# Squares of x added up in PSUM by VectorE, with the rotary angles, their sines and the low-rank Tanh emitted at other places

## The chip, the cores and the metric

One core of one Trainium2 chip runs the whole kernel. The metric is the device time of one execution in microseconds (us); less is better. Its engines are TensorE (PE, with its weight loads as PEld), VectorE (DVE), ScalarE (ACT), GpSimd (POOL) and SyncE (SP), whose queue issues all transfers. Each engine works through its own list in order and waits at semaphores for the others.

## The reference

One encoder layer with 1024 positions and a model width of 1024. What bears on this change is its beginning:

```python
h = rms_norm(x, norm_mix_g[l])                 # x * rsqrt(mean(x*x) + eps) * g
proj = h @ w_in[l]
mla_cols, rw_cols, gate_cols = _split(proj, [MLA_COLS, RWKV_COLS, GATE_COLS])
...
ang = positions.astype(jnp.float32)[..., None] * inv_freq
cos, sin = jnp.cos(ang).astype(x.dtype), jnp.sin(ang).astype(x.dtype)
...
q_rope = rope(rms_norm(q_rope, qr_g), cos[:, :, None, :], sin[:, :, None, :])
k_rope = rope(rms_norm(k_rope, kr_g), cos, sin)
...
a = jax.nn.sigmoid(a0 + a_lo @ a2)
w = -jax.nn.softplus(-(w0_d + jnp.tanh(dlo) @ w2_d)) - 0.5
```

Attention over all positions, a forward and a backward RWKV-7 scan, two output projections and a gated feed-forward layer follow.

## The kernel before, in words

Activations lie as features by positions, [128, 1024], in two halves of 512 positions (`HT`), each half one PSUM bank wide. Every product is made to nearly float32 accuracy by splitting both operands into a high and a low part: `whi` is a ScalarE cast of a weight tile, `wlo` the rest, computed by GpSimd, and each pair of halves takes six matmuls, hh*whi, hl*whi and hh*wlo for both halves. One "k step" below is such a group of six for one of the eight 128-row slices of x.

**The first stage** loads eight tiles `xt` of x. `ld` makes `hh` (ScalarE, x times the gain) and `hl` (VectorE, the rest). The reciprocal norm `rstd` isn't applied to x but to the products, when they leave PSUM (`evac`), so matmuls can start before it is known. `square(k)` squares a tile on ScalarE, and GpSimd adds the squares up in `acc` (named `xacc` in the trace). Step "s" of the list `XORDER` sums `acc` over the features with two float32 matmuls (`ss<-xacc`), and ScalarE makes `rstd` from it with a Ln and an Exp. `XORDER` also sets the order of TensorE's work: the tiles `T_CQ` (two) and `T_CKV`, with "s" between the second and the third. `rotary_tables` computes the angles of the rotary embedding on VectorE: some 18 instructions on [128, 1024], from a broadcast load of the positions, ending in a ScalarE Sin for `sinT` and one for `cosT`.

**The second stage** is one after another `inproj(T_L2)`, `inproj(T_L1)`, `inproj(T_GF)`, `inproj(T_GB)` and twelve more tiles. Their PSUM banks are three called `st` and one called `po`: `T_CQ` holds all four, so `T_L2`, which takes two of them, waits for `evac` of `T_CQ`. `l1_done` and `l2_done` shift the low-rank columns (tiles `l1` and `l2`) and put a Tanh on half of each. Between the k steps stand pieces of background generators: `norm_ckv`, `norm_cq`, `key_rope` (rotary key, tiles `sqk` and `rsk`, needs `cosT` and `sinT`), `rw_prep(p)` for four pairs of heads (first step "lora": matmuls `up<-l,a2w` and `up<-l,w2b`, then a ScalarE Sigmoid into `at` or `sg`), `mla_nope` (matmuls `up<-ck`, then `lift`: a Square `sqh` on ScalarE and a copy `q` on VectorE, then the sum `ss<-ghi`, `ss<-glo`), `mla_v` and `mla_rope`. Background products share two PSUM banks called `up`, sums share two called `ss`.

**The order.** TensorE's list is the order in which the program emits matmuls. Where a background piece stands is set by a clock that the program counts itself (`now`): a generator yields a name, and the table `DELAY` says how long after that its next piece may be emitted. The other engines' lists in these stages are made by the scheduler of the language, from dependences and its own estimates. From the scan on, all lists are written by hand.

A ScalarE function belongs to a table set, and `act` puts a table load where the set changes: Ln and Exp share one, Sigmoid and Tanh another, Sin a third. Squares, copies and scalings need none.

Of the kernel before, what the change touches and what calls it, by code (L numbers as in the profile page):

```python
# [54 lines left out]
CARRY = 3000  # L55
BATCH = 2500
DELAY = {
    "tab": 2100, "sum": 3900, "cq": 2040, "kr": 3100, "kr2": 750, "kr3": 0, "nope": 2975, "nope2": 1440,
    "rope": 541, "rope2": 5334, "rope3": 1470, "v": 805, "lora": 746, "kk": 10600, "kk2": 1785, "rk": 4080,
    "bo": 400,  # L60
}
# [25 lines left out]
def block_kernel(ctx: ExitStack, tc: tile.TileContext, a):  # L87
# [183 lines left out]
    onef = ap_.tile([128, 128], F32, name="onef")  # L271
    G.memset(onef, 1.0)
    G.tensor_copy(onesr, onef)
    HT = (slice(0, 512), slice(512, 1024))

    nst = [0]
# [27 lines left out]
    cqps = [big(), big()]  # L304
    ckps = [up1(), up1()]
    first3 = [*cqps, ckps]
    with pool("xp") as xp:
        xt = [xp.tile([128, T], F32, name=f"xt{k}") for k in range(8)]
        acc = xp.tile([128, T], F32, name="xacc")
        w3 = {}  # L310

        def wl3(t, h):
            raw = xp.tile([128, 512], F32, tag=f"raw{t}", name=f"raw{t}{h}")
            nc.sync.dma_start(raw, a["w_in"][t][:, h * 512:(h + 1) * 512])
            if h == 0:
                hi, lo = (xp.tile([128, 512], R, name=f"{n}{t}") for n in ("whi", "wlo"))
            else:
                hi, lo = (wpool["w"].tile([128, 512], R, tag=n, name=n, bufs=2) for n in ("whi", "wlo"))
            split(raw, hi, lo)
            w3[t, h] = hi, lo  # L320

        def ld(k):
            nc.sync.dma_start(xt[k], a["xT"][k * 128:(k + 1) * 128, :])
            hh, hl = hx[k]
            S.activation(hh, xt[k], AF.Copy, scale=vc("gmix", k))
            V.scalar_tensor_tensor(out=hl, in0=xt[k], scalar=vc("gmix", k), in1=hh.bitcast(F32), op0=mult, op1=sub)

        def square(k):
            if k == 0:
                S.activation(acc, xt[0], AF.Square)  # L330
            else:
                S.activation(xt[k], xt[k], AF.Square)
                G.tensor_tensor(out=acc, in0=acc, in1=xt[k], op=add)

        def mm(t, k):
            wh, wl = w3[t, k // 4]
            ws = slice(k % 4 * 128, (k % 4 + 1) * 128)
            mmk(first3[t], wh[:, ws], wl[:, ws], hx[k], k == 0, k == 7)

        def rotary_tables():  # L340
            posi = xp.tile([128, T], I32, name="posi")
            nc.sync.dma_start(posi, a["pos"].to_broadcast([128, T]))
            ang, kq = (xp.tile([128, T], F32, name=n) for n in ("ang", "kq"))
            V.tensor_copy(ang, posi)
            V.tensor_scalar(ang, ang, cst[:, C_FREQ:C_FREQ + 1], None, op0=mult)
            magic = 12582912.0
            for dst, off, fin in ((sinT, 0.0, 0.0), (cosT, 0.25, 0.5 * math.pi)):
                V.tensor_scalar(kq, ang, 1.0 / (2 * math.pi), off, op0=mult, op1=add)
                V.tensor_scalar(kq, kq, magic, -magic, op0=add, op1=add)
                src = ang  # L350
                rest = 2 * math.pi
                for bits in (8, 8, 8, 24):
                    if bits == 24:
                        cc = float(np.float32(rest))
                    else:
                        m, e = math.frexp(rest)
                        cc = math.ldexp(math.floor(m * 2 ** bits), e - bits)
                    rest -= cc
                    V.scalar_tensor_tensor(out=dst, in0=kq, scalar=-cc, in1=src, op0=mult, op1=add)
                    src = dst  # L360
                pi_ = 3.1415925
                if fin:
                    V.tensor_scalar(dst, dst, fin, pi_, op0=add, op1=ALU.min)
                    V.tensor_scalar(dst, dst, -pi_, None, op0=ALU.max)
                else:
                    V.tensor_scalar(dst, dst, pi_, -pi_, op0=ALU.min, op1=ALU.max)
                act(dst, dst, AF.Sin)

        for step in XORDER:
            if step[0] == "w":  # L370
                wl3(step[1], step[2])
            elif step[0] == "x":
                ld(step[1])
            elif step[0] == "q":
                square(step[1])
            elif step[0] == "r":
                rotary_tables()
            elif step[0] == "m":
                mm(step[1], step[2])
            else:  # L380
                for hs in HT:
                    ss = ss1()
                    E.matmul(ss, onef, acc[:, hs], start=True, stop=True)
                    rsqrt_(rstd[:, hs], ss, 1.0 / D, eps)
# [18 lines left out]

    for q, ps in zip([*cqs, ckv], first3):
        evac(q, ps)

    nc.sync.dma_start(a2w, a["w_l1"])
    for dst, src in ((b64r, a["consts"][:, C_B64:]), (b16, a["b16"])):
# [71 lines left out]
    def norm_cq():  # L480
        sq = [tt("sq") for _ in range(2)]
        for i in range(2):
            S.activation(sq[i], cqs[i], AF.Square)
        G.tensor_tensor(out=sq[0], in0=sq[0], in1=sq[1], op=add)
        pt = parted2(sq[0])
        yield "sum"
        rs = tt("rs")
        for x, hs in zip(pt, HT):
            rsqrt_(rs[:, hs], gsum(onesr, x), 1.0 / 256, eps)
        for i in range(2):  # L490
            V.scalar_tensor_tensor(out=cqs[i], in0=cqs[i], scalar=vc("gqa", i), in1=rs, op0=mult, op1=mult)
            split(cqs[i], cqh[:, i, :], cql[:, i, :], V)
        yield "cq"
# [143 lines left out]
    def rw_prep(p):  # L637
        cs = slice(p * 128, (p + 1) * 128)
        w2b = tp.tile([64, 128], F32, tag="w2b", name="w2b", bufs=2)
        nc.sync.dma_start(w2b, a["w_l2"][:, cs])  # L640
        at = keep(3, "at")
        for dst, wt, src, bias, key in (
            (at, a2w[0:64, cs], l1[0:64, :], vc("a0", p), None),
            (None, a2w[64:128, cs], l1[64:128, :], vc("w0f", p), "s0"),
            (None, w2b, l2[0:64, :], vc("w0b", p), "s1"),
        ):
            if dst is None:
                dst = tt("sg")
            for hs in HT:
                ps = up1()  # L650
                mul(ps, wt, src[:, hs], start=True, stop=True)
                act(dst[:, hs], ps, AF.Sigmoid, bias=bias)
                yield "lora"
            if key:
                nc.sync.dma_start(d_rw[key][:, p, :], dst)
        yield (p, 1)
        kt = rkv[p, 1]
        sq = tt("sq")
        S.activation(sq, kt, AF.Square, scale=vc("kk", p))
        pt = parted2(sq)  # L660
        kf = tt("kf")
        S.activation(kf, at, AF.Identity, scale=vc("ka", p), bias=ka1[:, p:p + 1])
        G.tensor_tensor(out=kf, in0=kf, in1=kt, op=mult)
        for h in range(2):
            nc.sync.dma_start(d_rw[("x2", "x1")[h]][H[h], p, :], kf[H[h], :])
        yield "kk"
        nr = tt("nr")
        for x, hs in zip(pt, HT):
            V.tensor_scalar(nr[:, hs], gsum(b64r, x), 1e-24, None, op0=ALU.max)
        act(nr, nr, AF.Ln, scale=float(2.0 ** KK_SHIFT))  # L670
        act(nr, nr, AF.Exp, scale=-0.5, bias=kkb)
        V.scalar_tensor_tensor(out=nr, in0=kt, scalar=vc("kk", p), in1=nr, op0=mult, op1=mult)
        nc.sync.dma_start(d_rw["kk"][:, p, :], nr)
        V.scalar_tensor_tensor(out=at, in0=at, scalar=-1.0, in1=nr, op0=mult, op1=mult)
        for h in range(2):
            nc.sync.dma_start(d_rw[("x1", "x2")[h]][H[h], p, :], at[H[h], :])
        yield "kk2"
        yield (p, 0)
        rk = kf
        V.scalar_tensor_tensor(out=rk, in0=rkv[p, 0], scalar=vc("rk", p), in1=kf, op0=mult, op1=mult)  # L680
        pt = parted2(rk)
        yield "rk"
        yield (p, 2)
        bo = tt("bo")
        for x, hs in zip(pt, HT):
            bs = gsum(b64r, x)
            V.tensor_tensor(out=bo[:, hs], in0=bs, in1=rkv[p, 2][:, hs], op=mult)
            yield "bo"
        S.activation(bo, bo, AF.Identity, bias=vc("lnb", p))
        nc.sync.dma_start(d_rw["bo"][:, p, :], bo)  # L690
# [11 lines left out]

    def l1_done(ps):
        shift(ps, 0, l1)
        act(l1[64:128, :], l1[64:128, :], AF.Tanh)

    def l2_done(ps):
        shift(ps, 1, l2)
        act(l2[0:64, :], l2[0:64, :], AF.Tanh)

    def gl_done(d):
        def done(ps):
# [1475 lines left out]
```

## Time and profile before

| | us |
|---|---|
| median of 3 runs | 1938.6 (1937.78 to 1941.22) |
| the profiled execution | 1937.92 |
| its span, first to last instruction | 1936.1 |
| TensorE busy in the span | 1841.8 (95%) |
| VectorE, ScalarE, GpSimd busy | 1229.6, 871.1, 655.4 |

The profiled execution lies 1.8 us above its span and 0.7 us below the median. A busy TensorE also counts time in which it ran at a lower clock; the granted clock is a column of the view of windows (1.00 is 2.4 GHz, 0.50 is 1.2 GHz).

### The profile page before, as it was taken

Reading aid. Unit: us, or ns where it says so; the run is one execution under the profiler, and the core shown is the slowest. Engines: PE = TensorE matmul, PEld = TensorE weight load, DVE = VectorE, ACT = ScalarE, POOL = GpSimd, SP = SyncE. Lnnn points to the kernel's source line nnn. Section 1 sums busy time; section 2 is a strip of 40 time slices with the busy share of each in tenths; the row PEclk is TensorE's granted clock in tenths of the full one; section 3 lists DMA queues with packets and bytes.
Section 4 is the critical chain, followed back from the end, with each engine's and each line's share of the span. In section 5 each row is a group of like instructions: output and inputs, shape, how many; then the busy total and the mean of one; then the engine's idle time right before and its main releaser. Section 6 shows DMA issues by size and latency. Waiting matters only on the chain. (4 is left out here: it accounts for less than half of the span.)

```text
span 1936.1 us, 36734 instructions
## 1 busy us (share of the span) xinstructions
PE 1841.8 (95%) x14928; PEld 1467.8 (76%) x14928; DVE 1229.6 (64%) x1837; ACT 871.1 (45%) x1380; POOL 655.4 (34%) x558
## 2 busy tenths in 40 slices
PE   6889999999999999989999999988999999999998
PEld 5657666888788877767777777767888888888886
DVE  7567665445556686766573264687766757667567
ACT  5676567223233565655666444442323333233231
POOL 7435554421222333352533322236222222222321
PEclk9989999999999999997999999999999999999999
DMA  4135544954555645453435672101111111111112
GB/s 158 37 120 193 181 157 147 252 140 99 142 144 122 148 110 137 101 139 84 104 83 174 213 250 87 55 33 55 50 56 59 49 50 52 63 50 50 49 55 103
DMA packets 260632, 210.65 MB, mean 109 GB/s; under 512 B 127144, under 2 KB 205032, under 8 KB 260464
## 3 DMA queue, kind: packets, MB, share of 16 engines
q1 hardware_dynamic: 260464, 208.31, 36.4%
q8 instruction: 117, 1.92, 0.4%
q14 instruction: 51, 0.42, 0.1%
HBM read 144.64 MB, written 59.41 MB: 105 GB/s over the span
## 5 line engine op out<-in xcount | busy, mean ns | idle before, releaser
L108 POOL TENSOR_TENSOR wlo<-wraw,whi 128x512 fp32r<-128x512 f32 x118 | 162.2, 1375 | 586.9 <-ACT whi L108 580.1
L123 PE MATMUL st<-hh,whi 128*128 128x512 f32 x408 | 172.4, 422 | 15.1 <-ACT hh L108 9.5
L123 PE MATMUL st<-hl,whi 128*128 128x512 f32 x408 | 163.6, 401 | 0.7 <-DVE hl L108 0.7
L108 DVE TENSOR_TENSOR x<-b,x 128x512 f32<-128x512 f32 x176 | 119.0, 686 | 54.9 <-PE b L123 54.9
L123 PE MATMUL st<-hh,wlo 128*128 128x512 f32 x408 | 140.3, 398 | 0.7 <-POOL wlo L108 0.7
L108 POOL TENSOR_TENSOR pl<-pe,ph 128x512 fp32r<-128x512 f32 x64 | 83.1, 1300 | 165.3 <-ACT ph L108 154.6
L108 ACT CAST whi<-wraw 128x512 fp32r<-128x512 f32 x118 | 72.9, 618 | 110.3 <-issue 30.4
L123 PEld LDWEIGHTS st<-hh,whi 128*128 128x128 f32 x408 | 78.9, 193 | 43.6 <-issue 10.9
L108 DVE TENSOR_REDUCE mx<-sc 128x1 f32<-128x512 f32 x128 | 81.8, 682 | 28.3 <-PE sc L123 28.1
L123 PEld LDWEIGHTS st<-hh,wlo 128*128 128x128 f32 x408 | 78.4, 192 | 19.1 <-POOL wlo L108 1.5
L123 PEld LDWEIGHTS st<-hl,whi 128*128 128x128 f32 x408 | 79.1, 194 | 17.7 <-DVE hl L108 1.6
L108 POOL TENSOR_TENSOR wl<-wraw,wh 128x512 fp32r<-128x512 f32 x22 | 28.9, 1313 | 179.7 <-ACT wh L108 174.8
L108 DVE TENSOR_TENSOR u<-b,p 128x512 f32<-128x512 f32 x42 | 29.0, 690 | 71.7 <-PE b L123 71.7
L123 PE MATMUL b<-sh,wh 128*128 128x512 f32 x176 | 69.3, 394 | 2.6 <-ACT sh L108 2.6
L123 PE MATMUL b<-sl,wh 128*128 128x512 f32 x176 | 69.1, 393 | 0.8 <-DVE sl L108 0.8
L123 PE MATMUL b<-sh,whi 128*128 128x512 f32 x176 | 68.6, 390 | 1.3 <-DVE x L108 1.3
L123 PE MATMUL b<-sh,wl 128*128 128x512 f32 x176 | 69.2, 393 | 0.0
L123 PE MATMUL b<-sh,wlo 128*128 128x512 f32 x176 | 68.5, 389 | 0.0
L123 PE MATMUL b<-sl,whi 128*128 128x512 f32 x176 | 68.5, 389 | 0.0
L108 DVE TENSOR_TENSOR pl<-st,ph 128x512 fp32r<-128x512 f32 x64 | 43.6, 683 | 28.3 <-ACT st L108 27.9
L108 ACT CAST whi<-s 128x512 fp32r<-128x512 f32 x33 | 20.5, 622 | 89.1 <-PE b L123 89.1
L123 PE MATMUL po<-ph,vhh 128*128 128x512 f32 x128 | 58.3, 455 | 1.8 <-ACT rc L108 1.8
(487 smaller groups left out, 5360.9 us busy)
## 6 DMA issues: line engine op xcount, KB each, us to landing
wraw<-w_in SPq DMA_DIRECT2D x64, 256.0 KB
wraw<-w_fd SPq DMA_DIRECT2D x44, 256.0 KB
AA<-w_fu SPq DMA_DIRECT2D x41, 256.0 KB
A<-w_fg SPq DMA_DIRECT2D x41, 256.0 KB
ld<-d_x SPq DMA_DIRECT2D x32, 256.0 KB
d_gate<-gt SPq DMA_DIRECT2D x32, 256.0 KB
xt<-xT SPq DMA_DIRECT2D x8, 512.0 KB
d_s<-sg SPq DMA_DIRECT2D x8, 512.0 KB
```

The costliest lines, as they stand in the source:

```text
L108: return f(*args, **kw)
L123: return f(out, a, b, **kw)
```

## The change

The eight squares of x are no longer added up in SBUF by GpSimd. ScalarE squares the first tile into two PSUM banks of the tag `ss`, and VectorE adds each half of the other seven squares to these banks; the last addition of each half writes `acc` in SBUF. A dependence is added so that the next table load comes behind the last square. The positions are loaded into the memory of `cosT`. The angles are emitted behind the evacuation of the first three tiles, with `ang` in the memory of `l1`. Both Sin move into `l2_done`. Both Tanh move into the first `rw_prep`, which then waits for 2500 (`"tanh"`) before its lora products; and `norm_cq` waits for 6000 (`"cq0"`) instead of 3900.

```diff
 DELAY = {
-    "tab": 2100, "sum": 3900, "cq": 2040, ...
+    "tab": 2100, "cq0": 6000, "tanh": 2500, "sum": 3900, "cq": 2040, ...
...
+    posi = cosT.bitcast(I32)
...
+    accps = [ss1(), ss1()]
...
         def square(k):
-            if k == 0:
-                S.activation(acc, xt[0], AF.Square)
-            else:
-                S.activation(xt[k], xt[k], AF.Square)
-                G.tensor_tensor(out=acc, in0=acc, in1=xt[k], op=add)
+            if k:
+                cur["group"] = [S.activation(xt[k], xt[k], AF.Square)]
+            for hs, p in zip(HT, accps):
+                if k == 0:
+                    S.activation(p, xt[0][:, hs], AF.Square)
+                else:
+                    V.tensor_tensor(out=p if k < 7 else acc[:, hs], in0=p, in1=xt[k][:, hs], op=add)
...
             elif step[0] == "r":
-                rotary_tables()
+                nc.sync.dma_start(posi, a["pos"].to_broadcast([128, T]))
...
     for q, ps in zip([*cqs, ckv], first3):
         evac(q, ps)
+    def rotary_tables():
+        ang, kq = l1, keep(3, "kq")
+        V.tensor_copy(ang, posi)
...
+    rotary_tables()
...
         pt = parted2(sq[0])
-        yield "sum"
+        yield "cq0"
...
         at = keep(3, "at")
+        if p == 0:
+            for x, r in ((l1, slice(64, 128)), (l2, slice(0, 64))):
+                act(x[r, :], x[r, :], AF.Tanh)
+            yield "tanh"
...
     def l1_done(ps):
         shift(ps, 0, l1)
-        act(l1[64:128, :], l1[64:128, :], AF.Tanh)

     def l2_done(ps):
+        for dst in (sinT, cosT):
+            act(dst, dst, AF.Sin)
         shift(ps, 1, l2)
-        act(l2[0:64, :], l2[0:64, :], AF.Tanh)
```

Three places show how the lists change. The first is VectorE's list around the evacuation of the first tiles (`cq` and `ckv` are evacuations; `kq`, `ang`, `sinT` and `cosT` the rotary angles). Before:

```order
L108 TENSOR_SCALAR kq<-kq 128x1024
L108 SCALAR_TENSOR_TENSOR cosT<-kq,ang 128x1024
L108 SCALAR_TENSOR_TENSOR cosT<-kq,cosT 128x1024 x3
L108 TENSOR_SCALAR cosT<-cosT 128x1024 x2
L108 TENSOR_TENSOR cq_449<-st,rstd 128x512
L108 TENSOR_TENSOR cq_450<-st,rstd 128x512
```

VectorE's list at the same place now (`ss` here is the PSUM bank in which the squares are added, `l_164` the angles in the memory of `l1`):

```order
L108 TENSOR_TENSOR ss<-ss,xt_189 128x512 x2
L108 TENSOR_TENSOR xacc<-ss,xt_190 128x512 x2
L108 TENSOR_SCALAR kq<-l_164 128x1024
L108 TENSOR_TENSOR cq_436<-st,rstd 128x512
L108 TENSOR_TENSOR cq_437<-st,rstd 128x512
L108 TENSOR_SCALAR kq<-kq 128x1024
L108 TENSOR_TENSOR cq_436<-st,rstd 128x512
L108 TENSOR_TENSOR cq_437<-po,rstd 128x512
L108 SCALAR_TENSOR_TENSOR sinT<-kq,l_164 128x1024
L108 SCALAR_TENSOR_TENSOR sinT<-kq,sinT 128x1024
L108 TENSOR_TENSOR ckv<-up,rstd 128x512 x2
```

The additions end ahead of the evacuations, and nearly all of the angles now stand behind them.

The second place is ScalarE's list around the key's norm (`rsk`) and the first Sigmoid (`at`). Before (`l_164<-l_164` is the Tanh of `l1`):

```order
L108 CAST ghi<-sqh 128x512
L108 ACTIVATE l_164<-l_164 64x1024
L108 ACT_TABLE_LOAD
L108 ACTIVATE rsk<-ss,cst 64x512 x2
L108 ACTIVATE rsk<-rsk 64x512 x2
L108 ACTIVATE sqh<-ss,cst 128x512
L108 ACTIVATE sqh<-sqh 128x512
L108 ACT_TABLE_LOAD
L108 CAST whi<-wraw 128x512
L108 CAST hi<-q 128x512
L108 ACTIVATE at<-up,vec 128x512
```

ScalarE's list there now (`l_164<-u` is the scaled copy that `shift` makes, `l_165` is `l2`):

```order
L108 CAST ghi<-sqh 128x512
L108 ACTIVATE l_164<-u,c_470 128x1024
L108 ACTIVATE rsk<-ss,cst 64x512 x2
L108 ACTIVATE rsk<-rsk 64x512 x2
L108 ACTIVATE sqh<-ss,cst 128x512
L108 CAST whi<-wraw 128x512
L108 ACTIVATE sqh<-sqh 128x512
L108 ACT_TABLE_LOAD
L108 ACTIVATE l_165<-l_165 64x1024
L108 CAST shi<-sraw 128x128
L108 ACTIVATE sqh<-up 128x512
L108 ACTIVATE l_164<-l_164 64x1024
```

The key's Ln has neither the Tanh nor its table load ahead of it any more; both Tanh stand between it and the first Sigmoid.

The third place is TensorE's list in `T_GF`, behind the key's sums. Before (`hh_143` is the fifth k step, `up<-l_164` a lora product, `up<-ck` the second product of `mla_nope`):

```order
L123 MATMUL st<-hh_141,wlo 128x512 x2
L123 MATMUL up<-l_164,a2w 128x512
L123 MATMUL up<-ckh,shi 128x512
L123 MATMUL up<-ckl,shi 128x512
L123 MATMUL up<-ckh,slo 128x512
L123 MATMUL st<-hh_143,whi 128x512
```

The same piece of TensorE's list now:

```order
L123 MATMUL st<-hh_143,wlo 128x512 x2
L123 MATMUL up<-ckh,shi 128x512
L123 MATMUL up<-ckl,shi 128x512
L123 MATMUL up<-ckh,slo 128x512
L123 MATMUL st<-hh_145,whi 128x512
L123 MATMUL st<-hl_146,whi 128x512
L123 MATMUL st<-hh_145,whi 128x512
L123 MATMUL st<-hl_146,whi 128x512
L123 MATMUL st<-hh_145,wlo 128x512 x2
L123 MATMUL up<-l_164,a2w 128x512
```

The lora products begin two k steps later, and the second product of `mla_nope` takes an `up` bank ahead of them. Behind this the background pieces stand a few matmuls earlier or later than before, and from the 1137th of TensorE's 10,756 matmuls on the list is the same.

## Rows read from the trace of the kernel before

**Rows 1.** What TensorE waited for from 0 to 360 us: total, times, longest (us).

```profile
PE st L123 <- DVE cq L108: 5.5, 1, 5.5
PE ss L123 <- POOL xacc L108: 4.6, 1, 4.6
...
PE ss L123 <- POOL plo L108: 3.9, 6, 1.5
...
PE st L123 <- DVE hl L108: 0.7, 2, 0.5
PE st L123 <- POOL wlo L108: 0.7, 2, 0.5
```

**Rows 2.** TensorE's timeline: start and length in us, instruction, [idle before <- releaser].

```profile
46.71 3.78 PE L123 MATMUL ss<-xacc,onef 128*128 128x512 f32 x4 [4.59 <-POOL xacc L108]
...
62.01 0.79 PE L123 MATMUL st<-hh,whi 128*128 128x512 f32 x1 [5.49 <-DVE cq L108]
...
66.35 0.39 PE L123 MATMUL st<-hh,whi 128*128 128x512 f32 x1
...
70.45 0.40 PE L123 MATMUL ss<-phi,onesr 128*128 128x512 f32 x1
...
94.68 1.93 PE L123 MATMUL ss<-sqk,onef 64*64 64x512 f32 x4
100.64 0.80 PE L123 MATMUL ss<-ghi,b64r 128*128 128x512 f32 x1 [4.03 <-ACT rsk L108]
...
111.16 0.50 PE L123 MATMUL st<-hh,whi 128*128 128x512 f32 x1
...
121.31 0.50 PE L123 MATMUL up<-ckh,shi 128*128 128x512 f32 x1 [1.73 <-ACT sg L108]
...
238.93 1.75 PE L123 MATMUL up<-l,a2w 64*128 64x512 f32 x2 [1.79 <-DVE q L108]
```

**Rows 3.** ScalarE's timeline, 57 to 100 us.

```profile
57.08 1.06 ACT L108 ACTIVATE cosT<-cosT 128x1024 f32<-128x1024 f32 x1 [7.76 <-DVE cosT L108]
58.16 1.28 ACT L108 ACT_TABLE_LOAD   x1
59.45 1.26 ACT L108 ACTIVATE rstd<-ss,cst 128x512 f32<-128x512 f32 x2
...
97.54 1.05 ACT L108 ACTIVATE l<-l 64x1024 f32<-64x1024 f32 x1 [0.72 <-DVE l L108]
98.61 1.28 ACT L108 ACT_TABLE_LOAD   x1
```

**Rows 4.** VectorE's timeline, 9 to 57 us.

```profile
9.45 1.28 DVE L108 SCALAR_TENSOR_TENSOR hl<-xt,vec,hh 128x1024 fp32r<-128x1024 f32 x1 [5.37 <-ACT hh L108]
...
13.52 15.43 DVE L108 SCALAR_TENSOR_TENSOR hl<-xt,vec,hh 128x1024 fp32r<-128x1024 f32 x5 [0.20 <-ACT hh L108]
...
55.53 1.52 DVE L108 TENSOR_SCALAR cosT<-cosT 128x1024 f32<-128x1024 f32 x2
```

**Rows 5.** VectorE's groups, 0 to 380 us: count, busy us, mean ns, idle before.

```profile
L108 DVE SCALAR_TENSOR_TENSOR hl<-xt,vec,hh 128x1024 fp32r<-128x1024 f32 x8 | 21.5, 2722 | 6.8 <-ACT hh L108 6.8
...
L108 DVE TENSOR_TENSOR u<-st,rstd 128x512 f32<-128x512 f32 x24 | 15.8, 684 | 30.9 <-PE st L123 30.9
...
L108 DVE TENSOR_TENSOR o<-o,t 128x512 f32<-128x512 f32 x4 | 6.0, 1498 | 2.4 <-POOL t L108 2.4
```

**Rows 6.** GpSimd's groups, 0 to 64 us.

```profile
L108 POOL TENSOR_TENSOR xacc<-xacc,xt 128x1024 f32<-128x1024 f32 x7 | 22.5, 3217 | 0.4
```

**Rows 7.** VectorE's groups over the whole run; `b` is a PSUM bank.

```profile
L108 DVE TENSOR_TENSOR b<-b,p 128x512 f32<-128x512 f32 x21 | 14.7, 698 | 6.3 <-PE b L123 6.3
```

**Rows 8.** ScalarE's groups, 0 to 380 us; the squares of `xt`.

```profile
L108 ACT ACTIVATE xt<-xt 128x1024 f32<-128x1024 f32 x7 | 7.4, 1059 | 8.6 <-DVE hl L108 8.5
```

**Rows 9.** Windows: length; PE, PEld, DVE, ACT, POOL busy (count); clock; DMA.

```profile
99.90:121.30 21.40, 18.94 (x47) 10.42 (x47) 14.72 (x14) 15.88 (x24) 7.95 (x6) 0.77 0.24 75
230.00:254.00 24.00, 21.48 (x56) 11.53 (x56) 12.89 (x13) 12.19 (x19) 12.55 (x9) 0.79 0.44 152
```

More of the change, by code (lines that the diff above doesn't have):

```diff
@@ L57 @@
 DELAY = {
-    "tab": 2100, "sum": 3900, "cq": 2040, "kr": 3100, "kr2": 750, "kr3": 0, "nope": 2975, "nope2": 1440,
+    "tab": 2100, "cq0": 6000, "tanh": 2500, "sum": 3900, "cq": 2040, "kr": 3100, "kr2": 750, "kr3": 0, "nope": 2975, "nope2": 1440,
     "rope": 541, "rope2": 5334, "rope3": 1470, "v": 805, "lora": 746, "kk": 10600, "kk2": 1785, "rk": 4080,
@@ L338, in mm @@
             mmk(first3[t], wh[:, ws], wl[:, ws], hx[k], k == 0, k == 7)
[L340 to L367, printed above, removed]
         for step in XORDER:
@@ L405, in block_kernel @@
         evac(q, ps)
+    def rotary_tables():
+        ang, kq = l1, keep(3, "kq")
+        V.tensor_copy(ang, posi)
+        V.tensor_scalar(ang, ang, cst[:, C_FREQ:C_FREQ + 1], None, op0=mult)
+        magic = 12582912.0
+        for dst, off, fin in ((sinT, 0.0, 0.0), (cosT, 0.25, 0.5 * math.pi)):
+            V.tensor_scalar(kq, ang, 1.0 / (2 * math.pi), off, op0=mult, op1=add)
+            V.tensor_scalar(kq, kq, magic, -magic, op0=add, op1=add)
+            src = ang
+            rest = 2 * math.pi
+            for bits in (8, 8, 8, 24):
+                if bits == 24:
+                    cc = float(np.float32(rest))
+                else:
+                    m, e = math.frexp(rest)
+                    cc = math.ldexp(math.floor(m * 2 ** bits), e - bits)
+                rest -= cc
+                V.scalar_tensor_tensor(out=dst, in0=kq, scalar=-cc, in1=src, op0=mult, op1=add)
+                src = dst
+            pi_ = 3.1415925
+            if fin:
+                V.tensor_scalar(dst, dst, fin, pi_, op0=add, op1=ALU.min)
+                V.tensor_scalar(dst, dst, -pi_, None, op0=ALU.max)
+            else:
+                V.tensor_scalar(dst, dst, pi_, -pi_, op0=ALU.min, op1=ALU.max)
+    rotary_tables()
     nc.sync.dma_start(a2w, a["w_l1"])
```

## The prediction

> **What bounds the kernel now.** TensorE is busy for 95% of the span, and its list is fixed. So I read first what TensorE waits for, then its timeline, to see after which waits it runs slowly, and last the lists of the engines it waits for. The change touches only the first 370 us. There the reader sees two large waits close together, 4.6 us for `xacc` and 5.5 us for `cq` [rows 1], a third of 4.0 us for `rsk` at 100.64, and smaller ones at 121.31 and 238.93 [rows 2]. Behind four of these waits the pace is half: from 62.01 to 66.35 TensorE does 12 matmuls in 4.34 us, from 66.35 to 70.45 it does 18 in 4.10, or 0.228 each [rows 2]. The slow pace is the lower of the clock's two levels, 1.2 GHz in place of 2.4. After the wait of 1.79 us at 238.93 it came too: the window around it has a mean clock of 0.79 [rows 9]. After the 1.73 us at 121.31 I read none.
>
> The causes stand in the other lists. `xacc` takes GpSimd 3.2 us per addition, seven times [rows 6], beside VectorE's `hl`, which takes 1.28 us alone and 2.72 in the mean [rows 4, 5]; ScalarE's squares wait 8.5 us for `hl` in turn [rows 8]. `cq` waits for `rstd`, and `rstd` stands on ScalarE behind the Sin of `cosT`, which waited until VectorE had computed its angles at 57.05, and behind a table load of 1.28 us [rows 3, 4]. `rsk` stands behind the Tanh of `l1`, which waited 0.72 us for VectorE, and a table load [rows 3].
>
> **The change part by part. The squares.** GpSimd loses seven additions of 3.2 us. VectorE gets fourteen on [128, 512], from and to PSUM with one operand in SBUF. The nearest row of this form takes 0.698 us [rows 7]; an addition of this size with both operands in SBUF beside GpSimd takes 1.50 [rows 5]. I take 0.70, because [rows 7] have the very form, and keep 1.50 for the range; less than 0.68 is seen for no [128, 512] form here. From 13.5 us on VectorE then has six `hl` at 1.28 (7.7), fourteen additions (9.8) and the cast and product of the angles at about 0.75 each (1.5): `xacc` is ready at about 32.5, at 1.50 each at 43.7. TensorE came to it at 42.1 (46.71 less 4.59), and arrives at 41.0 if the waits for `hl` and `wlo` go (0.7 and 0.7, of which about 0.3 stays, [rows 1]). So the wait of 4.6 us goes.
>
> GpSimd's additions and VectorE's `hl` slow each other, while VectorE's evacuations, which read PSUM and one SBUF operand, take 0.684 us in the mean of 24 [rows 5]. The Trainium skill (SBUF — State Buffer, "SBUF: two separate sides") says that a GpSimd instruction and a VectorE one with two SBUF inputs lock each other out of a shared port pair. By that rule the additions cost 0.70 us whatever GpSimd does, and `xacc` is ready at 32.5 as above; without it they might cost 1.50.
>
> **The angles and Sin.** Ahead of `rstd` on ScalarE there is no Sin any more, and the set of Ln and Exp is loaded long before. At the higher clock the two sums take about 1.9 us (the two at 94.68 do, [rows 2]) where they took 3.78. The first half is done at 42.0, its Ln takes 0.63 [rows 3] and its Exp about as long, and the second half follows. The four evacuations of 0.68 and one product of the angles are done by about 46.5. Meanwhile TensorE does the 24 matmuls of `T_CKV`: 41.0 + 1.9 + 24 x 0.228 = 48.4. So `T_L2` starts without a wait at 48.4, not 62.01, **13.6 us** earlier. It also has no slow start: 4.34 - 12 x 0.228 = **1.6 us** more. The angles, some 20 us of VectorE's time, then lie beside `T_L2`: VectorE must evacuate `T_L2` before `T_GF` takes its banks, a whole tile or 48 matmuls (11 us) after `T_L2`'s end at about 60. Even if the angles last until 65, nothing waits. What becomes late instead is the sum of `norm_ckv`, 30 matmuls into `T_L2` (55.2): its square, cast and GpSimd rest now run beside VectorE's angles. I take **-0.5 us**, between 0 and -2.
>
> The two Sin together cost ScalarE 2.1 us during `T_L2` and `T_L1`, as before; the one of `sinT` now stands ahead of `norm_cq`'s casts, whose sum TensorE wants one k step (1.4 us) later than before. These cancel: 0.
>
> **The Tanh.** `rsk` loses 0.72 + 1.05 + 1.28 = 3.05 us of waiting, Tanh and table load ahead of it [rows 3], and one more load (1.28) between Exp and Ln of the norms, since no Tanh stands between these. That is 4.3 us against a wait of 4.0, so the wait goes: **4.0 us**. With it goes the slow stretch behind it. From 100.64 to 111.16 there are 17 plain matmuls and two lora products; at 0.228, and half of the 1.93 us at 94.68 for each float32 product, these are 5.8 us instead of 10.5: **4.7 us** [rows 2].
>
> In exchange ScalarE becomes the limit behind it. From `rsk` to the Sigmoid that releases TensorE at 121.31 ScalarE was busy for 15.9 us [rows 9]. Now this stretch also holds two Tanh (2.1) and a scaled copy (1.1), and one Sigmoid less (0.7): 18.4, or 17.8 counted from the first Ln's end. TensorE's work up to the same product of `mla_nope` is 43 matmuls and four lora products, 43 x 0.228 + 4 x 0.97 = 13.7. It must wait the difference, 4.1, where it waited 1.7 at this place: **-2.4 us**. I see two places, the second lora product (its `up` bank is free only after VectorE's copy `q`, which now stands behind the key's rotary products) and the third `mla_nope` product (behind `sg`). Queued behind these is TensorE's whole list. That the clock stays at its higher level here is the choice I am least sure of: waits of 1.73 kept it, 1.79 lost it.
>
> **The order behind.** With `DELAY` moved, a `mla_rope` product now stands directly between two lora products near 220 us, and the three share two banks that VectorE's copies free; VectorE is late there already (the wait at 238.93). I take two such waits for one: **-1.8 us**; the slow stretch that follows stays.
>
> **Sum.** 13.6 + 1.6 - 0.5 + 4.0 + 4.7 - 2.4 - 1.8 = 19.2 us. From the profiled execution, 1937.9 (0.7 below the median), this gives 1918.7; I say 1918.5. From there to the end the lists are the same, so I carry the gain through.
>
> **The rivals.** (1) *The clock falls at the new waits.* If both new waits are followed by a stretch at 1.2 GHz as at 100.64, twice 4.7 us are lost: 1928. For it speak four waits that were followed by one; against it the wait at 121.31, and that ScalarE is the limit there, so a slower TensorE partly only fills its own waits. The Trainium skill (TensorE: Matmul & The Clock Gate, "The HAM clock gate") says that the low clock is the default and activity releases it; by that rule the scattered new waits may cost as much as a long one, and it gives the time of this rival.
>
> (2) *The banks work out better.* If the copies `q` come in time, the 4.1 and two times 1.8 us aren't lost, nor the slow stretch behind 238.93, (1 - 0.79) x 24 = 5.0 us [rows 9]: about 1918.5 - 4.1 - 3.6 - 5.0 = 1906. Against it speaks that both banks of `up` are asked for more tightly than before.
>
> (3) *VectorE is late with the additions.* At 1.50 us each TensorE waits 2.7 us for `xacc`, and the sums and `T_CKV` behind it run slow as they did (56.5 - 46.71 = 9.8 instead of 7.4, 2.4 us): 1923.5. [rows 7] speak against it.
>
> (4) *Slower: the lora waits recur.* `rw_prep` runs four times, and each time its lora products share the two `up` banks with `mla_nope` or `mla_rope`. If each pass, and the `mla_rope` place besides, has a wait and a slow stretch like those at 100.64 (4.0 + 4.7), the five cost 43.5 us, where before the places at 121.31 and 238.93 cost 1.7 + 1.8 + 5.0 = 8.5. Less the 2.4 + 1.8 already in the sum this adds 30.8: 1949. With four such places the gain is just gone (34.8 - 8.5 - 4.2 = 22.1, 1940.6). Only one of four passes shows it before.
>
> **How the numbers follow.** The forecast with its smaller terms (1912 to 1924) has 0.60, rival 1 0.17, rival 2 0.12, rival 3 0.05, rival 4 0.06, half of it with four places and half with five. The range of 1909 to 1929 leaves out part of rival 2 and all of rival 4. About 0.2%, 3.9 us, is what a measurement can tell from no change here. Faster by more: 0.94; within: 0.03; slower: 0.03.
>
> **What would show it.** VectorE's `ss<-ss,xt` at 0.70 us and `hl` near 1.3; TensorE's first long wait gone, its two `xacc` sums near 41 and taking 1.9 us; `T_L2` near 48.4; no wait for `rsk`; ScalarE without gaps from `rsk` to `sg`, and TensorE's waits for `q` and `sg` there, about 2 us each, with a window clock of 1.00. `T_L2` later than 52 would make the first half of the sum wrong; a clock below 0.9 between 85 and 110 us the second half.

## The result and the profile after

| | before | changed |
|---|---|---|
| median of 8 runs each (us) | 1938.39 (1933.19 to 1943.08) | 1925.92 (1921.68 to 1931.02) |
| ratio, 95% interval | | 0.9938 (0.9919 to 0.9957) |
| the profiled execution | 1937.92 | 1922.28 |
| first `Er<-sc` of the scan on VectorE (all lists are the same from here on) | 397.83 | 381.52 |

The change is faster by 12.5 us in the medians, 15.6 in the two profiled executions, where 19.4 were forecast. Two later comparisons of the same two kernels gave 10.6 and 10.2 us (ratios 0.9943 and 0.9950).

The head of the page of the changed kernel:

```profile
span 1920.5 us, 36727 instructions
...
PE 1828.2 (95%) x14928; PEld 1462.8 (76%) x14928; DVE 1219.7 (64%) x1851; ACT 865.7 (45%) x1377; POOL 631.9 (33%) x551
```

TensorE is as busy as before, and GpSimd has lost the seven additions, 655.4 to 631.9 us. What TensorE waited for from 0 to 360 us in the changed kernel (total, times, longest), against [rows 1]:

```profile
PE ss L123 <- POOL glo L108: 8.4, 6, 2.6
PE ss L123 <- POOL plo L108: 6.1, 4, 3.4
PE up L123 <- DVE q L108: 1.6, 1, 1.6
...
PE st L123 <- DVE hl L108: 0.5, 1, 0.5
PE up L123 <- ACT sg L108: 0.4, 1, 0.4
```

`xacc`, `cq` and `rsk` are gone from the list; two names that were small, `plo` and `glo`, lead it. TensorE's timeline of the changed kernel, against [rows 2]:

```profile
39.79 1.88 PE L123 MATMUL ss<-xacc,onef 128*128 128x512 f32 x4
...
46.99 0.39 PE L123 MATMUL st<-hh,whi 128*128 128x512 f32 x1
...
68.05 0.50 PE L123 MATMUL ss<-plo,onesr 128*128 128x512 f32 x1 [3.39 <-POOL plo L108]
...
69.72 0.80 PE L123 MATMUL ss<-plo,onesr 128*128 128x512 f32 x1 [0.94 <-POOL plo L108]
...
83.25 1.93 PE L123 MATMUL ss<-sqk,onef 64*64 64x512 f32 x4
85.11 0.50 PE L123 MATMUL ss<-ghi,b64r 128*128 128x512 f32 x1
...
96.84 0.80 PE L123 MATMUL ss<-glo,b64r 128*128 128x512 f32 x1 [1.70 <-POOL glo L108]
...
104.14 0.50 PE L123 MATMUL up<-ckh,shi 128*128 128x512 f32 x1 [0.44 <-ACT sg L108]
```

`T_L2` starts at 46.99 instead of 62.01, with no wait and at 0.39 us for its first matmul, the pace of the higher clock. The sums behind the key's norm follow without a wait for `rsk`. New is the wait of 3.39 us at 68.05. GpSimd's timeline names its cause, and VectorE's beside it shows where that stood:

```profile
61.67 2.03 POOL L108 TENSOR_TENSOR wlo<-wraw,whi 128x512 fp32r<-128x512 f32 x1 [1.47 <-ACT whi L108]
66.72 2.95 POOL L108 TENSOR_TENSOR plo<-sq,phi 128x512 fp32r<-128x512 f32 x2 [3.02 <-DVE ckv L108]
```

```profile
57.87 6.92 DVE L108 SCALAR_TENSOR_TENSOR cosT<-kq,cosT 128x1024 f32<-128x1024 f32 x3
64.70 0.68 DVE L108 TENSOR_TENSOR u<-st,rstd 128x512 f32<-128x512 f32 x1
65.31 1.27 DVE L108 SCALAR_TENSOR_TENSOR ckv<-ckv,vec,rs 128x1024 f32<-128x1024 f32 x1
```

`plo` of `norm_cq` is written into one of three buffers of the tag `tp`, the one that held `rs` of `norm_ckv`; VectorE's `ckv` is its last reader, and it stands behind three 2.3 us products of `cosT`. VectorE's groups to 45 us give the cost of the additions, 0.68 us each, against [rows 5] and [rows 7]; `hl` is down from 2722 to 1507 ns:

```profile
L108 DVE SCALAR_TENSOR_TENSOR hl<-xt,vec,hh 128x1024 fp32r<-128x1024 f32 x8 | 11.9, 1507 | 6.6 <-ACT hh L108 6.6
L108 DVE TENSOR_TENSOR ss<-ss,xt 128x512 f32<-128x512 f32 x12 | 7.6, 682 | 0.0
```

Windows of the changed kernel, columns as in [rows 9]; the last number but two is the clock:

```profile
66.00:86.00 20.00, 17.01 (x56) 12.14 (x57) 16.30 (x15) 14.57 (x19) 7.91 (x5) 0.83 0.08 27
96.00:106.00 10.00, 8.72 (x25) 5.34 (x26) 9.11 (x10) 9.82 (x14) 3.01 (x3) 0.83 0.53 162
```

Behind the waits at 68 and 96.84 the clock is 0.83, which costs (1 - 0.83) x 20 = 3.4 and (1 - 0.83) x 10 = 1.7 us. The first of these costs isn't fixed. The same window in two later profiles of the same kernel (after_again, then after_third), behind the same waits of 3.4 and 0.9 us, has 0.91, or 1.8 us:

```profile
66.00:86.00 20.00, 16.82 (x60) 12.15 (x61) 17.09 (x15) 15.80 (x21) 7.96 (x5) 0.91 0.08 27
66.00:86.00 20.00, 16.48 (x59) 11.77 (x60) 17.09 (x15) 15.51 (x20) 7.95 (x5) 0.91 0.10 32
```

The slow stretch that [rows 9] show behind the wait for `q` is gone in the first profile: that wait now lies at 223.53, and the window 220 to 230 us has a clock of 1.00 (shown below).

### The profile page after: what moved, and what is told of

Same layout as the page of the kernel before. It is cut to its first block, busy times and chain, and to the rows that moved or that the text cites. A ratio compares the mean times of both kernels' runs of the same rounds, so it can differ in the third digit from the quotient of the medians.

```text
span 1920.5 us, 36727 instructions
## 1 busy us (share of the span) xinstructions
PE 1828.2 (95%) x14928; PEld 1462.8 (76%) x14928; DVE 1219.7 (64%) x1851; ACT 865.7 (45%) x1377; POOL 631.9 (33%) x551
## 4 chain that ended last, share of the span: by engine, by line
PE 40%; DVE 6%; ACT 2%; DMA 1%; issue 1%; POOL 0%; SPq 0%; ACTq 0%; DVEq 0%; POOLq 0%
PE b L123 35%; PE st L123 2%; DVE x L108 1%; PE sc L123 1%; PE po L123 1%; DVE u L108 1%; DVE gt L108 1%; DMA gt<-d_gate 1%; PE ct L123 0%; DVE wl L108 0%; DVE yl L108 0%; DVE wlo L108 0%; DVE b L108 0%; DVE cvb L108 0%; DVE RR L108 0%
```

## The experiments

My theory: two waits stood ahead of `T_L2`, one for the squares and one for Sin, and the Tanh made a third for `rsk`; the new loss is the buffer that `ckv` holds. The rivals: one part alone did it, or GpSimd and ScalarE are late by themselves. All runs with their places (us) are in this table; "gain at Er" is 397.83 less the start of `Er<-sc` in that run's trace.

| run | `T_L2` | gain at Er | median | ratio to before (95%) |
|---|---|---|---|---|
| changed, three profiles | 46.99, 47.19, 47.53 | 16.3, 13.8, 14.1 | 1925.92, 1928.44, 1929.60 | 0.9938, 0.9943, 0.9950 |
| squares_only | 55.83 | 5.7 | 1932.51 | 0.9959 (0.9940 to 0.9977) |
| no_squares | 49.18 | 10.1 | 1933.05 | 0.9969 (0.9950 to 0.9987) |
| gpsimd_one_load | 51.16 | 12.6 | 1931.17 | 0.9943 (0.9923 to 0.9962) |
| squares_sbuf | 47.54 | 14.7 | 1927.64 | 0.9944 (0.9922 to 0.9967) |
| no_tanh | 48.03 | 14.9 | 1930.12 | 0.9941 (0.9923 to 0.9958) |
| rs_own | 46.76 | 16.7 | 1925.88 | 0.9931 (0.9909 to 0.9953) |
| ckv_first | 46.07 | 10.5 | 1932.31 | 0.9977 (0.9958 to 0.9997) |
| cq0_9600 | 46.89 | 15.3 | 1929.60 | 0.9952 (0.9934 to 0.9970) |
| tp4 | 47.57 | 18.2 | 1919.23 | 0.9887 (0.9866 to 0.9907) |
| tp4_cq0_9600 | 47.23 | 20.8 | 1915.90 | 0.9885 (0.9858 to 0.9913) |

**Only the squares moved.** The kernel before with `square(k)` of the change:

```diff
+    accps = [ss1(), ss1()]
...
-                G.tensor_tensor(out=acc, in0=acc, in1=xt[k], op=add)
+                    V.tensor_tensor(out=p if k < 7 else acc[:, hs], in0=p, in1=xt[k][:, hs], op=add)
```

> Only the squares are added up in PSUM by VectorE; the angles, both Sin and both Tanh stay where the kernel before has them. Theory A (the squares and the place of Sin are two separate waits): the wait of 4.6 us for xacc goes, TensorE's sums over xacc start near 41, and hl takes 1.3 us. rstd still stands on ScalarE behind the Sin of cosT; VectorE's angles end near 49 in place of 57.05, since GpSimd slows VectorE no longer, so rstd starts near 51 and T_L2 near 53.5 in place of 62.0, with a wait of about 5 us for cq left and the slow clock behind it. Time about 1930 (8.5 us below the kernel before). Theory B (the whole gain in front of T_L2 is the place of Sin, the angles are as late as before): T_L2 at 60 to 62, time within 2 us of the kernel before. Theory C (the squares alone were it): T_L2 near 47, time near 1922.

The wait for `xacc` went, and that for `cq` grew to 8.16 us. ScalarE's timeline of this kernel shows the same chain as [rows 3], 6.2 us earlier: Sin of `cosT`, table load, then `rstd`.

```profile
50.91 1.06 ACT L108 ACTIVATE cosT<-cosT 128x1024 f32<-128x1024 f32 x1 [2.99 <-DVE cosT L108]
51.97 1.28 ACT L108 ACT_TABLE_LOAD   x1
53.27 1.27 ACT L108 ACTIVATE rstd<-ss,cst 128x512 f32<-128x512 f32 x2
```

Theory A holds, 2.3 us later than sized, mostly because `cosT` was ready at 50.9 and not at 49: VectorE's last products of the angles took 1.57 us each (4.71 for three), not 1.23 as the first one did.

**Everything but the squares.** The changed kernel with GpSimd adding in SBUF, first as the kernel before writes it:

```diff
-                cur["group"] = [S.activation(xt[k], xt[k], AF.Square)]
...
-                    V.tensor_tensor(out=p if k < 7 else acc[:, hs], in0=p, in1=xt[k][:, hs], op=add)
+                S.activation(xt[k], xt[k], AF.Square)
+                G.tensor_tensor(out=acc, in0=acc, in1=xt[k], op=add)
```

> The changed kernel with the squares added up by GpSimd in SBUF again; angles, Sin and Tanh stay where the change has them. In this program ScalarE's Ln and Exp of rstd get a table load each (four in place of one), which makes rstd up to 3.8 us later than it need be. Theory A (the two waits ahead of T_L2 are separate, each part removes one): the wait for xacc of 4.6 us comes back, TensorE's sums start near 46.5 and run slowly, with T_CKV behind them; there is no wait for cq, or a short one for the loads, and T_L2 starts at 55 to 59, between the kernel before (62.0) and the changed one (47.0): 1928 to 1932. Theory B (the place of Sin is nearly all of it, since VectorE is as late either way): T_L2 near 50, 1922 to 1925. Theory C (without the squares the rest is worth nothing): T_L2 at 61 or later, 1936 to 1938.

Theory A was wrong about `T_L2`, B right about it, and the time (1933.05) is above both. TensorE's timeline of this kernel:

```profile
41.87 1.98 PE L123 MATMUL ss<-xacc,onef 128*128 128x512 f32 x4 [0.81 <-POOL xacc L108]
...
49.18 0.39 PE L123 MATMUL st<-hh,whi 128*128 128x512 f32 x1
```

The wait for `xacc` is 0.81 us, not 4.6, though GpSimd does all seven additions. GpSimd's last two, in the kernel before and then in this one:

```profile
37.22 2.84 POOL L108 TENSOR_TENSOR slo<-sraw,shi 128x128 fp32r<-128x128 f32 x2
40.02 6.63 POOL L108 TENSOR_TENSOR xacc<-xacc,xt 128x1024 f32<-128x1024 f32 x2
```

```profile
36.12 0.88 POOL L108 TENSOR_TENSOR slo<-sraw,shi 128x128 fp32r<-128x128 f32 x2
36.95 4.87 POOL L108 TENSOR_TENSOR xacc<-xacc,xt 128x1024 f32<-128x1024 f32 x2
```

This execution is 0.8 us early from its first transfers on. The rest is VectorE's angles, which no longer run beside (VectorE is idle here from 34.7 to 45.7 us): 2.0 us less for `slo` and 1.8 for the additions, 3.8 together, and so most of the wait for `xacc`. The run loses its lead behind `T_L2`: `rstd` has four table loads and is whole at 49.6 instead of 43.4. So the loads had to be taken out:

```diff
+                cur["group"] = [S.activation(xt[k], xt[k], AF.Square)]
+                G.tensor_tensor(out=acc, in0=acc, in1=xt[k], op=add)
```

> The squares added up by GpSimd in SBUF, all else as in the changed kernel, and with the dependence that keeps the table load behind the last square, so that Ln and Exp of rstd have one load in place of four. Theory A (once the angles stand behind the evacuation, VectorE's additions are worth little; what the previous run without them lost was the loads): the wait for xacc is about 0.8 us, rstd is whole at 46, T_L2 starts near 49 without a wait, no wait for phi or plo near 57 to 60, and at 130 us TensorE is 1 to 3 us behind the changed kernel: 0 to 3 us slower than it. Theory B (VectorE's additions are worth 5 to 6 us by themselves): waits for phi and plo near 57 as with the four loads, 5 us or more behind at 130 us.

There is no wait for `xacc`, `phi` or `plo` up to 60 us, but ScalarE now casts a `whi` later, TensorE waits 1.59 us for it at 36.32 and runs slowly, and `T_L2` starts at 51.16. From there TensorE is 4.2 us behind the first trace of the changed kernel, 3.7 us at 130 us: Theory A, a little above its size. Between the times (1931.17 and 1929.60, measured together) no difference can be told.

**VectorE adds in SBUF.**

```diff
-            for hs, p in zip(HT, accps):
-                ...
+                V.tensor_tensor(out=acc, in0=acc, in1=xt[k], op=add)
```

> The changed kernel with the squares added up by VectorE in SBUF: seven additions of 128x1024 with both operands in SBUF in place of fourteen of 128x512 from and to PSUM. Theory A (what counts is that GpSimd no longer adds; PSUM gives nothing): an addition takes 1.2 to 1.3 us, xacc is ready near 32, T_L2 starts near 47, time within 2 us of the changed kernel. Theory B (PSUM is what keeps VectorE's additions fast): additions of 2 to 3 us wherever GpSimd works, hl slower too, xacc ready at 40 to 44, a wait for it of up to 4 us and a slow start of T_CKV, T_L2 at 48 to 52, 2 to 5 us slower than the changed kernel.

VectorE's group in this kernel is Theory A:

```profile
L108 DVE TENSOR_TENSOR xacc<-xacc,xt 128x1024 f32<-128x1024 f32 x7 | 8.8, 1264 | 0.2
```

1264 ns for 1024 columns is less than two of 682 in PSUM, and `T_L2` starts at 47.54. What PSUM does give is room for GpSimd. The same five GpSimd instructions of the stretch 13 to 33 us are busy for 5.22 us in the changed kernel and 8.98 here. The Trainium skill (SBUF — State Buffer, "SBUF: two separate sides") has the rule for it: two SBUF operands on VectorE lock GpSimd out, and the traces agree. Nobody waits for GpSimd there, and no difference in time is seen.

**The Tanh back.** The changed kernel with each Tanh behind its `shift` again:

```diff
     def l1_done(ps):
         shift(ps, 0, l1)
+        act(l1[64:128, :], l1[64:128, :], AF.Tanh)
```

> The changed kernel with the two Tanh back where the kernel before has them, right behind l1 and l2. Theory A (Tanh and its table loads ahead of rsk are a wait of their own): T_L2 stays near 47, the wait for rsk of about 4 us and a window at the lower clock behind it come back (8.7 us together), and the waits for glo at 96.84 and for sg at 104.14 with the slow stretch behind the first go (4 us): about 1927, 4 to 6 us above the changed kernel. Theory B (with both Sin gone from ScalarE ahead of it the Tanh is early enough): no wait over 1 us for rsk, time within 2 us of the changed kernel or below it.

TensorE's only large wait between 71 and 160 us in this kernel:

```profile
92.84 0.79 PE L123 MATMUL ss<-ghi,b64r 128*128 128x512 f32 x1 [7.62 <-ACT rsk L108]
```

The wait came back, larger than the 4.03 of [rows 2], since TensorE is there earlier, and the window 90 to 100 us has a clock of 0.50. The third `mla_nope` product starts at 111.83 instead of 104.14, 7.7 us later. At `Er` (382.92) this kernel lies among the three traces of the changed one (381.52, 384.00, 383.77), and by the medians (1930.12) nothing can be told: behind 112 us it has none of the waits for `glo` at 130 and 153. Theory A for the mechanism, but a net gain of the Tanh's move isn't shown.

**The buffer of `rs`.**

```diff
     def norm_ckv():
-        rs = tt("rs")
+        rs = tt("rs", "rsk", 1)
```

> The changed kernel with rs of norm_ckv in a buffer of its own in place of one of the three of the tag tp. Nothing else moves; TensorE's order is the same. Theory A (the wait of 3.39 us for plo at 68.05 is a wait for that buffer, which VectorE's ckv gives back only behind the angles of cosT): GpSimd's plo no longer waits for ckv but starts at about 63.7, TensorE's two waits for plo fall from 4.3 to about 2 us, and if the wait stays below 1.7 us the clock stays at 1.00 in the window 66 to 86 (3.4 us more): 2 to 5.6 us faster than the changed kernel, 1917 to 1920. Theory B (GpSimd itself is late, the angles on VectorE slow it through the shared memory port): plo as late as before, no change in time.

GpSimd's `plo` no longer waits:

```profile
61.26 2.08 POOL L108 TENSOR_TENSOR wlo<-wraw,whi 128x512 fp32r<-128x512 f32 x1 [1.41 <-ACT whi L108]
63.30 4.46 POOL L108 TENSOR_TENSOR plo<-sq,phi 128x512 fp32r<-128x512 f32 x2
```

So the buffer was the cause (Theory A). But `plo` now runs beside VectorE's `cosT` and takes 2.2 us instead of 1.5, which is Theory B's part; the two waits are 1.15 and 1.48 us. The clock from 66 to 86 us is 0.91 all the same, though neither wait reaches 1.7 us. At the first `mla_nope` product (76.58) TensorE is 3.1 us ahead of the first trace of the changed kernel; since that clock is also the one of the changed kernel's two later profiles, the buffer's own share is the 1.7 us by which the two waits fell. At the third product 0.9 us are left: there are waits for `rsk` (0.53) and `glo` (1.93, where the changed kernel has 1.70), and the clock from 85 to 110 us is 0.86. No difference in time is seen.

**`ckv` ahead of the angles.** Besides, `kq` of `cosT` gets that same buffer, so the angles can't start before `ckv` has read `rs`, and the angles of `cosT` are emitted in `l2_done`:

```diff
+        if dst is cosT:
+            kq = tt("kq2", "rsk", 1)
...
     def l2_done(ps):
+        rotary_table(cosT, 0.25, 0.5 * math.pi)
```

> The changed kernel with rs of norm_ckv in a buffer of its own, and with kq of cosT's angles in that same buffer, so that VectorE works on cosT's angles only behind ckv. TensorE's order is the same. Theory A (the angles are work of the path, wherever they stand): the waits for plo near 68 fall from 4.3 to 2 us or less, but cosT's angles end at 73 to 77 in place of 70, its Sin goes back with them, norm_cq's Ln and rsk stand behind that Sin on ScalarE, and a wait for rsk of 2 to 6 us comes back near 82: time within 3 us of the changed kernel, or above it. Theory B (the angles have slack): no wait for rsk over 1 us, 3 to 6 us faster than the changed kernel.

Theory A, with a larger wait, one instruction ahead of `rsk`:

```profile
83.52 3.67 PE L123 MATMUL ss<-sqk,onef 64*64 64x512 f32 x4 [7.47 <-ACT sqk L108]
```

The one wait for `plo` is 0.94 us, but the Sin of `cosT` starts at 78.77 instead of 70.25, and norm_cq's Ln, `sqk` and `rsk` follow it. At the third `mla_nope` product this kernel is 5.3 us behind the changed one. The angles have no slack in either place. But this order also leaves VectorE idle for 5.42 us ahead of `ckv`, waiting for `rs`; an order without that gap wasn't tried.

**TensorE asks later, and four buffers.** One number in `DELAY`, then `bufs=4` in `tt`, then both:

```diff
-    "tab": 2100, "cq0": 6000, ...
+    "tab": 2100, "cq0": 9600, ...
...
-    def tt(n, tag="tp", bufs=3, dtype=F32, w=T):
+    def tt(n, tag="tp", bufs=4, dtype=F32, w=T):
```

> The changed kernel with DELAY cq0 at 9600 in place of 6000: TensorE's four products of norm_cq stand three k steps (18 matmuls, 4.1 us) later in its list, nothing else moves. Theory A (the two waits for plo are only a matter of when TensorE asks): they fall from 4.3 us to under 1 and the slow stretch behind them goes (3.4), so TensorE is up to 7 us earlier at 80 us; but ScalarE's chain from the Sin of cosT at 70 to rsk at 84 does not start earlier, so a wait for rsk of 3 to 5 us comes back, and 2 to 4 us are left: 1918 to 1920. Theory B (norm_cq's later products delay its own chain on ScalarE and VectorE): rsk later than 85.1 us, time equal to the changed kernel or above it.

> The changed kernel with four buffers in place of three in the tag tp, the one for the half-norms and the small products. TensorE's order is the same. Theory A (the new waits for plo and glo are waits for buffers): as with rs_own the waits for plo near 68 fall to about 2 us, and the clearing of z on GpSimd no longer waits for VectorE's last use of rsk, so the wait of 1.70 us for glo at 96.84 and the lower clock behind it (1.7 us) go as well: 5 to 9 us faster than the changed kernel, 1914 to 1917. Theory B (the engines are late by themselves): waits move by less than 1 us each, time within 2 us of the changed kernel.

> Four buffers in the tag tp and DELAY cq0 at 9600 together. Theory A (the two answer different waits): no wait for plo near 66 to 70, no wait for glo near 95; what is left are waits for rsk and for sg on ScalarE, of 4 and 3.6 us. 0 to 4 us faster than with four buffers alone, 1910 to 1914 where that was 1914 by its profile. Theory B (ScalarE's list between 70 and 104 us is the limit, whatever TensorE waits for ahead of it): the third mla_nope product stays at 103.5, as with four buffers alone, and the time is within 1.5 us of it.

With the later demand alone the waits for `plo` fell to 0.56 us and TensorE was 4.1 us ahead at 75.6, but behind that place waits for `rsk` (0.59), `glo` (0.73 and 1.46) and `sg` (2.69), where the changed kernel has 1.70 and 0.44, took all but 0.5 us by 104. So neither theory holds as a whole: the waits for `plo` fell as A says, but the wait for `rsk` is 0.59 and not 3 to 5 us, and `rsk` isn't later, as B has it (TensorE's sum behind it starts at 81.61). Its profile ended at 1935.79, 13.5 us above the first of the changed kernel; at `Er` it was 1.0 behind, so 12.5 of these arose in lists that are the same. With four buffers TensorE's waits behind 60 us, up to 130 us, are:

```profile
PE up L123 <- ACT sg L108: 3.6, 1, 3.6
PE ss L123 <- POOL plo L108: 2.6, 2, 1.5
PE ss L123 <- ACT rsk L108: 2.0, 1, 2.0
PE ss L123 <- POOL glo L108: 0.3, 1, 0.3
```

The wait for `glo` went, since GpSimd clears `z` at 83.26 and no longer behind VectorE's `rsk`; one for `sg` took its place, and the third `mla_nope` product (103.53) is only 0.6 us earlier. More comes behind: 1.9 us at `Er`, 4.3 and 4.1 against the two later traces of the changed kernel. A part of this is the clock: its two waits for `plo` are those of rs_own (1.16 and 1.48 us), but the window 66 to 76 us has 1.00. With both edits that product starts at 100.87, against Theory B, and `Er` is 4.5 us earlier than in the first trace of the changed kernel; Theory A's waits for `rsk` and `sg` of some 4 us aren't there either (0.53 for `rsk`). Both versions beat both kernels: 0.9887 and 0.9885, with intervals below that of the changed kernel; between the two there is no difference to be told. Their medians lie 20 and 23 us below the kernel before, their traces at `Er` 18.2 and 20.8.

**The changed kernel again.**

> The changed kernel once more, nothing edited. Theory A (what differs between the forecast and the median beyond 370 us is scatter from execution to execution): TensorE's waits up to 360 us come back within 0.1 us each, but places between 700 and 1200 us stand 2 to 5 us away from where the first profile has them, in either direction. Theory B (the later part is as fixed as the first): every place within 0.5 us of the first profile over the whole span.

> The changed kernel a third time, on the chip of the run beside it, to compare with it and to see the scatter: waits up to 216 us within 0.1 us of the first profile, the clock behind the waits at 216 to 224 us at 1.00 or lower, time 1922 to 1930.

Nearly all waits up to 216 us came back within 0.1 us. The 0.44 us for `sg` at 104.14 came in neither, and in the second profile a wait for `glo` at 163 (1.14) stands for one for `phi` in the first (0.59). The window 220 to 230 us in the first profile and in the second, behind the same waits of 0.98, 0.83 and 1.58 us:

```profile
220.00:230.00 10.00, 8.41 (x27) 4.37 (x27) 8.89 (x10) 5.26 (x9) 6.91 (x6) 1.00 0.59 206
```

```profile
220.00:230.00 10.00, 8.42 (x18) 3.96 (x16) 7.91 (x10) 4.42 (x7) 5.75 (x5) 0.68 0.47 165
```

That is 3.2 us from one execution to the next. From `Er` to the end of the span the three took 1539.0, 1543.1 and 1540.7 us, the kernel before 1538.3, four buffers 1533.9 and the late demand 1551.4, all with the same lists. Theory A in the main; but the clock differs already behind waits that came back the same, at 68 us.

## Why the prediction was right, and where its sizes were off

Point by point, by TensorE's starts in the first traces of both kernels; the last column has the same steps by the second and third trace of the changed kernel:

| step | places | forecast | measured | later traces |
|---|---|---|---|---|
| `T_L2` earlier, no slow start, `norm_ckv` late | 70.45 to 53.80 | 14.7 | 16.65 | 16.5, 16.1 |
| sums of `norm_cq` | 91.15 to 79.72 | 0 | -5.2 | -4.0, -4.0 |
| wait for `rsk` | 100.64 to 85.11 | 4.0 | 4.1 | 4.1, 4.1 |
| slow stretch, less new waits, to the third `mla_nope` product | 121.31 to 104.14 | 2.3 | 1.6 | 0.2, 0.0 |
| order behind it, to `Er` | 397.83 to 381.52 | -1.8 | -0.9 | -2.9, -2.2 |
| from there to the end of the span | 1936.1 to 1920.5 | 0 | -0.7 | -4.8, -2.4 |
| sum | | 19.2 | 15.6 | 9.0, 11.6 |

The direction and the place of the gain were right: the first and the third step came in every trace. The additions cost 0.68 us, where 0.70 was taken from [rows 7], `xacc` was ready near 32, TensorE's sums started at 39.79, 1.2 us ahead of the 41.0 in the sum, and took 1.88 us, and `norm_ckv` came in time, so nothing was lost for the 0.5 set aside. The size was less sure than the range makes it look. The median of 1925.92 lies in the range of 1909 to 1929, but above the 1912 to 1924 that the forecast's own terms allowed, and nearer to rival 1's 1928 than to 1918.5.

**The step that failed** is the one for `norm_cq`, "These cancel: 0", with its ground, "Even if the angles last until 65, nothing waits". I had looked at who waits for the evacuation of `T_L2` and for Sin, not at what else stands behind the angles on VectorE. There it is `ckv`, which holds a buffer that GpSimd's next `plo` needs. The angles also lasted until 70: beside GpSimd a product of `cosT` took 2.3 us and not the 1.23 of the first. It cost 2.4 us of waiting (4.33 against 1.93), and what remains, 2.8, is slow clock (3.4 by the window, partly under the waits); in the two later traces, with a clock of 0.91 there, 1.6 remain. rs_own shows the buffer as the cause of GpSimd's wait of 3.02 us, and ckv_first that the one other order tried on VectorE doesn't cure it.

**A right sum with a partly wrong reason.** I gave the wait for `xacc` to the additions on GpSimd beside `hl`. no_squares shows that the angles beside the last additions made 3.8 of its 4.6 us. Apart, the squares bring `T_L2` 6.2 us forward and the rest of the change 10.9 with one table load for `rstd` and 12.8 with four; together they bring 15.0. At `Er` the rest is worth 12.6 and the squares on top of it 1.2 to 3.7, by the three traces of the changed kernel. In the medians the squares' part can't be seen.

**The Tanh.** The wait for `rsk` went and no_tanh brought it back. The new waits were taken for the copies `q` and for `sg`, 4.1 us; they came as 0.17 (`at`), 1.70 (`glo`, behind the clearing of `z`) and 0.44 (`sg`), 2.3 in all, and with a slow stretch of 1.7. The prediction gave a clock below 0.9 between 85 and 110 us as the sign that this half is wrong. The first profile, then the second and the third:

```profile
85.00:110.00 25.00, 22.67 (x71) 13.11 (x70) 19.77 (x19) 21.25 (x31) 7.88 (x7) 0.93 0.41 136
85.00:110.00 25.00, 23.03 (x68) 12.61 (x66) 20.57 (x19) 20.54 (x29) 8.05 (x7) 0.86 0.41 136
85.00:110.00 25.00, 23.03 (x62) 12.79 (x61) 20.91 (x20) 20.32 (x30) 8.05 (x7) 0.80 0.38 119
```

So the term for the slow stretch, 4.7 us, with the choice that the clock stays high behind the new waits, held in the first execution, by luck, and not in the other two: there the step is worth 0.2 and 0.0 us in place of 2.3. The wait of 4.0 for `rsk` went in all three.

**The order behind.** One wait for `q` of 1.59 us came at 223.53, not two, and the slow stretch that I had let stand went in this execution. In the second execution it came back (0.68 in the window shown above). In exchange `glo` is waited for at 130, 153, 260 and 273 us, 0.6 to 2.6 us each. Rival 1 was half right: in the first profile the clock fell behind the waits at 68 and 96.84, at a cost of 5.1 us, but these were waits for `plo`, which no rival named, and for `glo`, not for `q` and `sg`. Rival 4's waits didn't come in every pass of the lora products: of the waits over 1 us the passes hold those at 96.84 and 223.53, and the four for `glo` stand between passes. Rivals 2 and 3 didn't come: some waits stayed, and no addition took longer than 0.7 us.

**The rest of the gap**, from 15.6 in the profiles to 10 to 12.5 in the medians, is explained only in part: the first profiled execution of the changed kernel lies near the lower end of its runs (1922.28 of 1921.68 to 1931.02), and its other traces have 13.8 and 14.1 at `Er`. From `Er` to the end the thirteen other traces, the changed kernel's three among them, are on average 2.8 us longer than the one trace of the kernel before. Whether that is more than the scatter of that one trace stays open.

## What to carry to other kernels

When work moves to a busy engine, list what stands behind it there and which buffers these instructions give back; the next wait can be on a third engine that only needs the buffer. A wait named after one operation may be made by another that runs beside it: remove each suspect alone before the credit is given. And try one buffer more before reordering: here one number took the ratio to the kernel before from 0.9938 to 0.9950 down to 0.9887.

## What the runs showed of the hardware

TensorE's clock did not follow the length of the wait alone. Behind the wait of 1.58 to 1.59 us for `q` near 223 the window 220 to 230 us had 1.00 in the first and the third profile of the changed kernel and 0.68 in the second; rs_own, with the same wait, had 0.83. With waits for `plo` of 1.15 and 1.48 us rs_own had 0.83 in the window 66 to 76 us; with 1.16 and 1.48 us tp4 had 1.00 there. The wait of 2.56 us at 152.80 was followed by 0.83 in the first profile, and one of 2.62 at the same place in the second by 1.00. The Trainium skill (TensorE: Matmul & The Clock Gate, "The HAM clock gate") says that the number of slow matmuls at a kernel's start varies between runs of one kernel; these traces show such a variation in the middle of one too. The three profiled executions of the changed kernel (1922.28, 1928.88, 1926.26) lie up to 6.6 us apart, so a single one can't confirm a term of 2 us that hangs on the clock.

On VectorE a TENSOR_SCALAR, which reads a single operand in SBUF, is slowed beside GpSimd too. VectorE's timeline of the changed kernel, while GpSimd worked on `plo` and `wlo`:

```profile
53.09 1.78 DVE L108 TENSOR_SCALAR kq<-l 128x1024 f32<-128x1024 f32 x1
54.90 1.67 DVE L108 TENSOR_SCALAR kq<-kq 128x1024 f32<-128x1024 f32 x1
```

The same two took 0.68 and 0.69 us in the kernel before, at 47.12, where GpSimd stood idle. The fourteen additions of the squares, with one operand in PSUM, took 0.67 to 0.69 us each, some of them beside GpSimd.
